# Reordering the 256-column matmuls of a split-precision decoder layer on TensorE

## The chip, the cores and the metric

The kernel runs on one core of one Trainium2 chip. The metric is the device time of one execution in microseconds (us), lower is better. Times per instruction are in nanoseconds (ns).

## The reference

One decoder layer on 256 tokens of width 2048, all in float32. Four large products carry the work, with smaller work between them:

```python
u   = x @ w_in                       # first product:  (256,2048) @ (2048,6160)
mix = concat(conv_group(u), gated_deltanet(u)) @ w_out      # second product
x   = layer_norm(alpha * x + mix)
gu  = x @ w_gate_up                  # third product:  (256,2048) @ (2048,11264)
hid = silu(gu[..., :5632]) * gu[..., 5632:]
out = layer_norm(alpha * x + hid @ w_down)                  # fourth product
```

## The kernel before

Each float32 operand of a large product is split into a rounded part `hi` and a remainder `lo`, and a product is the sum of three TensorE products: hi\*hi, hi\*lo and lo\*hi. Weights come from memory in chunks of 256 rows by 512 columns (512 KB): SyncE issues the load into `wraw` (three buffers), ScalarE copies it to `whi` (L93), VectorE subtracts to get `wlo` (L100); `whi` and `wlo` have four buffers each.

The first product is done in 12 groups of 512 output columns. A group has eight chunks, a chunk two row blocks of 128 (`k2`) and four column blocks (`ct`). The output of `ct` lies in half of a PSUM bank, 256 tokens wide, so that a group uses two banks, `g1a` and `g1b`, of a pool of four. For each row block and column block three matmuls of 256 columns follow one another into the same half bank (L206 whi with x_hi, L208 whi with x_lo, L209 wlo with x_hi): 24 matmuls a chunk. Between two chunks a planner (`tick`) places side work of the small mixers on TensorE; their times come from a table written by hand. All of it is ordered after the last matmul of the chunk (`last[0]`).

The third product is done in 22 groups (`j`) of 512 columns. The normed x is kept as `x1`, with hi and lo side by side, so that one matmul of 512 columns takes whi with both parts (L840, `g3_hi`); hi and lo land in the two halves of a whole bank, and a group has four banks, `g3a` to `g3d`. Per chunk come eight such matmuls over the four banks in turn, and then eight of 256 columns for wlo with the hi part (L849, `g3_lo`). At the end of a group ScalarE copies the lo half of each bank (L890), VectorE adds the hi half (L891), then Silu (L894), the product (L895) and the split into `hid` (L896, L897). Group 0 is a special case: its first six chunks are taken in two halves of 128 tokens, filled in around the norm and its transposes (L798), and so have 256-column matmuls at L840 too; its last two chunks are as in the other groups. The second and fourth products use matmuls of 512 columns (L715 to L717), three in a row into one bank.

Of the kernel before, what the change touches and what calls it, by code (L numbers as in the profile page):

```python
# [7 lines left out]
F32 = mybir.dt.float32  # L8
F32R = mybir.dt.float32r
AF = mybir.ActivationFunctionType  # L10
ALU = mybir.AluOpType
# [3 lines left out]
P = 128  # L15
D = 2048
S = 256
KT = D // P
# [5 lines left out]
NG3 = FF // 256  # L24
# [36 lines left out]
def hybrid_layer(ctx: ExitStack, tc, xT, xn, w1, wba, w2, w3, w4, pvec, consts, hrow, lrow, out):  # L61
    nc = tc.nc
    TT = nc.vector.tensor_tensor
    STT = nc.vector.scalar_tensor_tensor
    TS = nc.vector.tensor_scalar
    ACT = nc.scalar.activation
    MM = nc.tensor.matmul
# [9 lines left out]
    def ps(name="ps"):  # L77
        return sd.tile([P, 512], F32, tag="sd", name=name)

    def mmt(name="mmt"):  # L80
        return mm.tile([P, 512], F32, tag="mm", name=name)
# [3 lines left out]
    def wload(src, split=False, into=None):  # L85
        with tc.high_priority(offset=WPRI):
            raw = into[2] if into and len(into) > 2 else wp.tile([P, 2, 512], F32, tag="wraw", name="wraw", bufs=3)
            hi = into[0] if into else wp.tile([P, 2, 512], F32R, tag="whi", name="whi")
            lo = into[1] if into else wp.tile([P, 2, 512], F32R, tag="wlo", name="wlo")
            parts = (0, 1) if split else (slice(0, 2),)  # L90
            for k in parts:
                loads[0] = nc.sync.dma_start(raw[:, k], src[:, k])
                ACT(hi[:, k], raw[:, k], AF.Copy)  # L93
        return raw, hi, lo, parts

    def wrest(w):
        raw, hi, lo, parts = w
        with tc.high_priority(offset=WPRI):
            for k in parts:
                TT(lo[:, k], raw[:, k], hi[:, k].bitcast(F32), op=ALU.subtract)  # L100
        return hi, lo

    def wchunk(src, split=False, into=None):
        return wrest(wload(src, split, into))
# [67 lines left out]
    last = [None]  # L172
# [12 lines left out]
    def tick():  # L185
        while todo and todo[0][0] <= clock[0]:
            run_next()
        clock[0] += 1
# [7 lines left out]
    def gemm_ws(banks, chunks, r_hi, r_lo, pre=None):  # L196
        for c in range(8):
            if pre is not None:
                pre(c)
            hi, lo = wchunk(chunks[c], split=(pre is not None and c < 2))  # L200
            for k2 in range(2):
                kt = 2 * c + k2
                for ct in range(4):
                    o = banks[ct // 2][:, (ct % 2) * S:(ct % 2) * S + S]
                    wsl = slice(ct * P, ct * P + P)
                    MM(o, lhsT=hi[:, k2, wsl], rhs=r_hi[:, kt, :], start=(kt == 0 and ct % 2 == 0),  # L206
                       stop=False, skip_group_check=True)
                    MM(o, lhsT=hi[:, k2, wsl], rhs=r_lo[:, kt, :], start=False, stop=False, skip_group_check=True)  # L208
                    last[0] = MM(o, lhsT=lo[:, k2, wsl], rhs=r_hi[:, kt, :], start=False, stop=(kt == KT - 1),  # L209
                                 skip_group_check=True)  # L210
            if c < 7:
                tick()

# [207 lines left out]
    for s in (32, 64):  # L421
        for hf in range(2):
            w = pb.tile([P, 4, P], F32, name=f"wz{s}_{hf}")
# [277 lines left out]
    for gi, (kind, idx, _) in enumerate(GROUPS):  # L701
        banks = [mmt("g1a"), mmt("g1b")]
        gemm_ws(banks, w1[gi], x_hi, x_lo, pre=first_loads if gi == 0 else None)
        {"kq": do_kq, "v": do_v, "conv": do_conv, "z": do_z}[kind](banks, idx)
        if gi == 0:
            at(clock[0] + 1, gates)
        tick()
# [17 lines left out]
    def gemm2(pas, nb):  # L725
        banks = [mmt("g2a"), mmt("g2b")]
        for c in range(4):
            hi, lo = wchunk(w2[pas, nb, c])
            require(("gc"[pas], c // 2))
            for k2 in range(2):  # L730
                for tk in range(2):
                    tok_mm(banks[tk], act_c if pas else act_g, 2 * c + k2, tk, hi, lo, k2, 8)
            tick()
        return banks
# [10 lines left out]
    for nb in range(4):  # L745
        banks = gemm2(0, nb)
# [19 lines left out]
    for nb in range(2):  # L766
        banks = gemm2(1, nb)
# [3 lines left out]
    x1 = [big.tile([P, KT // 2, 2, S], F32R, tag="big", name=f"x1_{i}") for i in range(2)]  # L771
# [61 lines left out]
    def g3_banks():  # L833
        return [mmt("g3a"), mmt("g3b"), ps("g3c"), ps("g3d")]

    def g3_hi(banks, w, c, tsl):
        for k2 in range(2):
            kt = 2 * c + k2
            for ct in range(4):
                m = MM(banks[ct].rearrange("p (a b) -> p a b", a=2)[:, :, tsl], lhsT=w[:, k2, ct * P:ct * P + P],  # L840
                       rhs=x1[kt // 8][:, kt % 8, :, tsl], start=(kt == 0 and tsl.start == 0), stop=False,
                       skip_group_check=True)
        return m

    def g3_lo(banks, w, c, tsl):
        for k2 in range(2):
            kt = 2 * c + k2
            for ct in range(4):
                last[0] = MM(banks[ct][:, tsl], lhsT=w[:, k2, ct * P:ct * P + P], rhs=x1[kt // 8][:, kt % 8, 0, tsl],  # L849
                             start=False, stop=(kt == KT - 1), skip_group_check=True)  # L850

    t0, t1 = slice(0, P), slice(P, S)
    banks3 = g3_banks()
# [22 lines left out]
    p2 = ctx.enter_context(tc.tile_pool(name="p2", bufs=1))  # L876

    hid = p2.tile([P, 2, FT, S], F32R, name="hid")
    for j in range(NG3):
        banks = g3_banks() if j else banks3  # L880
        for c in range(0 if j else NF, 8):
            hi, lo = wchunk(w3[j, c])
            g3_hi(banks, hi, c, slice(0, S))
            g3_lo(banks, lo, c, slice(0, S))
        gu = []
        for i in range(2):
            g = p2.tile([P, 2, S], F32, tag="t2k2", name="g3s", bufs=5)
            for k in range(2):
                bank = banks[2 * i + k]
                ACT(g[:, k, :], bank[:, S:2 * S], AF.Copy)  # L890
                TT(g[:, k, :], g[:, k, :], bank[:, 0:S], op=ALU.add)  # L891
            gu.append(g)
        sg, hv = gu
        ACT(sg, sg, AF.Silu)  # L894
        TT(hv, sg, hv, op=ALU.mult)  # L895
        ACT(hid[:, 0, 2 * j:2 * j + 2, :], hv, AF.Copy)  # L896
        TT(hid[:, 1, 2 * j:2 * j + 2, :], hv, hid[:, 0, 2 * j:2 * j + 2, :].bitcast(F32), op=ALU.subtract)  # L897
    st2 = cp.tile([P, 2, 4, 6], F32, name="st2")
# [22 lines left out]
    for nb in range(4):  # L921
        banks = [mmt("g4a"), mmt("g4b")]
        held = 6 if nb == 3 else 0
        for c in range(NC4 - held):
            hi, lo = wchunk(w4[nb, c])
# [20 lines left out]
NF = 6  # L946
# [83 lines left out]
```

## Time and profile before

| what | value |
|---|---|
| median of 3 runs | 1180.29 us (1179.14 to 1182.05) |
| profiled execution, span from its first to its last instruction | 1178.9 us |
| TensorE matmul busy | 1161.0 us, 98% |
| TensorE weight load busy | 1033.0 us, 88% |
| VectorE busy | 763.2 us, 65% |
| ScalarE busy | 585.1 us, 50% |
| memory traffic over the span | 188 GB/s |

The profiled execution has no time of its own beside its span; the median of the runs is 1.4 us above that span. PE is TensorE's matmul row and PEld its weight load, which runs beside the matmuls. A matmul's recorded length is longer than its share of the engine, since matmuls overlap: the pace is the distance from one start to the next.

### The profile page before, as it was taken

How to read it: one execution, taken by the hardware profiler on the slowest of the kernel's cores; microseconds unless marked ns; L12 is line 12 of the kernel's file. 1: busy time of each engine (PE TensorE's matmuls, PEld its weight loads, DVE VectorE, ACT ScalarE, POOL GpSimd, SP SyncE). 2: the span in 40 equal slices, each digit the busy share in tenths (PEclk: the TensorE clock that was granted, in tenths of full speed). 3: DMA queues.
4: the chain of work that ended last, by engine and by line, in shares of the span. 5: the costliest groups of instructions: out<-in, count | busy, mean ns of one | idle time of the engine just before them, and what ended most of it. 6: DMA issues, size and time to landing. Idle time of an engine off the chain costs nothing.

```text
span 1178.9 us, 18212 instructions
## 1 busy us (share of the span) xinstructions
PE 1161.0 (98%) x7170; PEld 1033.0 (88%) x7170; DVE 763.2 (65%) x1176; ACT 585.1 (50%) x887; POOL 34.9 (3%) x44
## 2 busy tenths in 40 slices
PE   9999999999999999999999999999999999999996
PEld 8999999999988879888888888888888888888884
DVE  5998998978757687555555555555555545454546
ACT  6567555556765455454454454454444433333340
POOL 1001011000000000000000000000000000000000
PEclk9999999999999999999999999999999999999998
DMA  8667675564645746666666666666666766666662
GB/s 290 176 185 217 180 208 155 151 197 126 204 138 178 249 142 184 208 190 190 192 186 190 193 188 190 192 188 193 187 191 193 250 196 189 190 193 193 188 204 94
DMA packets 62005, 222.50 MB, mean 189 GB/s; under 512 B 7168, under 2 KB 7680, under 8 KB 61280
## 3 DMA queue, kind: packets, MB, share of 16 engines
q1 hardware_dynamic: 58464, 208.37, 58.9%
q0 software_dynamic: 2160, 10.88, 2.9%
q10 hardware_dynamic: 1296, 2.10, 0.5%
q8 instruction: 56, 0.92, 0.3%
q14 instruction: 29, 0.24, 0.1%
HBM read 216.86 MB, written 4.46 MB: 188 GB/s over the span
## 4 chain that ended last, share of the span: by engine, by line
PE 92%; DMA 4%; ACT 1%; DVE 1%; issue 1%; POOL 0%; DVEq 0%; ACTq 0%
PE g3d L840 7%; PE g3b L840 7%; PE g3c L840 7%; PE g3a L840 7%; PE g3a L849 3%; PE g1a L206 3%; PE g4b L717 3%; PE g1a L208 3%; PE g4a L717 3%; PE g1b L209 3%; PE g1a L209 3%; PE g1b L208 3%; PE g1b L206 3%; PE g4a L716 3%; PE g4b L716 3%; PE g3d L849 3%
## 5 line engine op out<-in xcount | busy, mean ns | idle before, releaser
L100 DVE TENSOR_TENSOR wlo<-wraw,whi 128x1024 fp32r<-128x1024 f32 (+1 forms) x386 | 469.8, 1218 | 367.5 <-ACT whi L93 365.7
L93 ACT ACTIVATE whi<-wraw 128x1024 fp32r<-128x1024 f32 (+1 forms) x386 | 407.0, 1055 | 490.9 <-PE g3d L840 211.5
L840 PE MATMUL g3d<-x,whi 128*128 128x512 f32 (+1 forms) x356 | 139.8, 393 | 0.0
L840 PE MATMUL g3b<-x,whi 128*128 128x512 f32 (+1 forms) x356 | 139.7, 393 | 0.0
L840 PE MATMUL g3c<-x,whi 128*128 128x512 f32 (+1 forms) x356 | 138.0, 388 | 0.0
L840 PE MATMUL g3a<-x,whi 128*128 128x512 f32 (+1 forms) x356 | 137.5, 386 | 0.0
L206 PE MATMUL g1a<-x_hi,whi 128*128 128x256 f32 x384 | 110.6, 288 | 1.1 <-ACT x_hi L143 0.6
L208 PE MATMUL g1a<-x_lo,whi 128*128 128x256 f32 x384 | 107.9, 281 | 0.1
L209 PE MATMUL g1a<-x_hi,wlo 128*128 128x256 f32 x384 | 107.5, 280 | 0.0
L206 PE MATMUL g1b<-x_hi,whi 128*128 128x256 f32 x384 | 107.5, 280 | 0.0
L209 PE MATMUL g1b<-x_hi,wlo 128*128 128x256 f32 x384 | 107.4, 280 | 0.0
L208 PE MATMUL g1b<-x_lo,whi 128*128 128x256 f32 x384 | 107.4, 280 | 0.0
L641 DVE SCALAR_TENSOR_TENSOR cacc<-hh,pv,cacc 128x255 f32<-128x255 f32 (+27 forms) x240 | 100.0, 462 | 0.7 <-ACT cacc L638 0.7
L849 PE MATMUL g3a<-x,wlo 128*128 128x256 f32 x348 | 96.9, 278 | 0.0
L849 PE MATMUL g3d<-x,wlo 128*128 128x256 f32 x348 | 96.1, 276 | 0.0
L849 PE MATMUL g3b<-x,wlo 128*128 128x256 f32 x348 | 96.0, 276 | 0.0
L849 PE MATMUL g3c<-x,wlo 128*128 128x256 f32 x348 | 96.0, 276 | 0.0
L840 PEld LDWEIGHTS g3d<-x,whi 128*128 128x128 f32 x356 | 66.9, 188 | 16.3
L840 PEld LDWEIGHTS g3c<-x,whi 128*128 128x128 f32 x356 | 66.9, 188 | 13.6
L206 PEld LDWEIGHTS g1a<-x_hi,whi 128*128 128x128 f32 x384 | 72.7, 189 | 1.8 <-ACT x_hi L143 1.0
L840 PEld LDWEIGHTS g3b<-x,whi 128*128 128x128 f32 x356 | 66.9, 188 | 8.1
L840 PEld LDWEIGHTS g3a<-x,whi 128*128 128x128 f32 x356 | 66.9, 188 | 7.5 <-DVE x L802 0.2
(307 smaller groups left out, 2129.6 us busy)
## 6 DMA issues: line engine op xcount, KB each, us to landing
wraw<-in_w SPq DMA_DIRECT2D x388, 512.0 KB, 4.2
y<-in_xn POOLq DMA_DIRECT2D x1, 2048.0 KB, 9.6
rows<-in_lrow POOLq DMA_DIRECT2D x2, 1024.0 KB, 11.6
l<-in_lrow POOLq DMA_DIRECT2D x2, 1024.0 KB, 10.3
out<-y SPq DMA_DIRECT2D x8, 256.0 KB, 2.5
xr<-in_xT ACTq DMA_DIRECT2D x7, 256.0 KB, 5.4
wraw<-in_w SPq DMA_DIRECT2D x4, 256.0 KB, 4.1
dzx<-zbg POOLq DMA_DIRECT2D x2, 512.0 KB, 5.2
```

Of the source, the lines that this page charges most:

```text
L93: ACT(hi[:, k], raw[:, k], AF.Copy)
L100: TT(lo[:, k], raw[:, k], hi[:, k].bitcast(F32), op=ALU.subtract)
L206: MM(o, lhsT=hi[:, k2, wsl], rhs=r_hi[:, kt, :], start=(kt == 0 and ct % 2 == 0), stop=False, skip_group_check=True)
L208: MM(o, lhsT=hi[:, k2, wsl], rhs=r_lo[:, kt, :], start=False, stop=False, skip_group_check=True)
L209: last[0] = MM(o, lhsT=lo[:, k2, wsl], rhs=r_hi[:, kt, :], start=False, stop=(kt == KT - 1), skip_group_check=True)
L641: STT(a[:, s:], hh[:, i, :S - s], pcol(w + TAPS - 1 - s), a[:, s:], op0=ALU.mult, op1=ALU.add)
L716: MM(bank, lhsT=a_hi[:, tsl], rhs=lo[:, k2, :], start=False, stop=False)
L717: last[0] = MM(bank, lhsT=a_lo[:, tsl], rhs=hi[:, k2, :], start=False, stop=(kt == n - 1))
L840: m = MM(banks[ct].rearrange("p (a b) -> p a b", a=2)[:, :, tsl], lhsT=w[:, k2, ct * P:ct * P + P], rhs=x1[kt // 8][:, kt % 8, :, tsl], st ...
L849: last[0] = MM(banks[ct][:, tsl], lhsT=w[:, k2, ct * P:ct * P + P], rhs=x1[kt // 8][:, kt % 8, 0, tsl], start=False, stop=(kt == KT - 1), ...
```

## The change

In the first product the 24 matmuls of a chunk are put in another order: all eight hi\*hi over the four half banks in turn, for both row blocks, then the eight hi\*lo, then the eight lo\*hi. In the third product, groups 1 to 21, the 512-column matmul is replaced by two of 256 columns in the same order, and both land in one half bank, so that a group takes two banks instead of four. With that the copies and additions at the end of a group fall away: Silu reads its bank directly, and VectorE multiplies by the other bank. Group 0 of the third product, the second and the fourth product stay as they are.

```diff
-            for k2 in range(2):
-                kt = 2 * c + k2
-                for ct in range(4):
-                    o = banks[ct // 2][:, (ct % 2) * S:(ct % 2) * S + S]
-                    wsl = slice(ct * P, ct * P + P)
-                    MM(o, lhsT=hi[:, k2, wsl], rhs=r_hi[:, kt, :], start=(kt == 0 and ct % 2 == 0),
-                       stop=False, skip_group_check=True)
-                    MM(o, lhsT=hi[:, k2, wsl], rhs=r_lo[:, kt, :], start=False, stop=False, skip_group_check=True)
-                    last[0] = MM(o, lhsT=lo[:, k2, wsl], rhs=r_hi[:, kt, :], start=False, stop=(kt == KT - 1),
-                                 skip_group_check=True)
+            for w, r, fin in ((hi, r_hi, False), (hi, r_lo, False), (lo, r_hi, True)):
+                for k2 in range(2):
+                    kt = 2 * c + k2
+                    for ct in range(4):
+                        o = banks[ct // 2][:, (ct % 2) * S:(ct % 2) * S + S]
+                        last[0] = MM(o, lhsT=w[:, k2, ct * P:ct * P + P], rhs=r[:, kt, :],
+                                     start=(kt == 0 and ct % 2 == 0 and r is r_hi and not fin),
+                                     stop=(fin and kt == KT - 1), skip_group_check=True)
...
+    def g3_evac(banks):
+        sg = p2.tile([P, 2, S], F32, tag="t2k2", name="g3s", bufs=5)
+        ACT(sg.rearrange("p a b -> p (a b)"), banks[0], AF.Silu)
+        hv = p2.tile([P, 2, S], F32, tag="t2k2", name="g3h", bufs=5)
+        return sg, banks[1].rearrange("p (a b) -> p a b", a=2), hv
+
+    def g3_chunk(banks, hi, lo, c):
+        for w, part, fin in ((hi, 0, False), (hi, 1, False), (lo, 0, True)):
+            for k2 in range(2):
+                kt = 2 * c + k2
+                for ct in range(4):
+                    last[0] = MM(banks[ct // 2][:, (ct % 2) * S:(ct % 2) * S + S], lhsT=w[:, k2, ct * P:ct * P + P],
+                                 rhs=x1[kt // 8][:, kt % 8, part, :],
+                                 start=(kt == 0 and ct % 2 == 0 and part == 0 and not fin),
+                                 stop=(fin and kt == KT - 1), skip_group_check=True)
+
+    for j in range(NG3):
+        banks = [mmt("g3a"), mmt("g3b")] if j else banks3
+        for c in range(0 if j else NF, 8):
+            hi, lo = wchunk(w3[j, c])
+            if j:
+                g3_chunk(banks, hi, lo, c)
+            else:
+                g3_hi(banks, hi, c, slice(0, S))
+                g3_lo(banks, lo, c, slice(0, S))
+        sg, up, hv = g3_evac(banks) if j else g3_evac0(banks)
+        TT(hv, sg, up, op=ALU.mult)
```

`g3_evac0` is the old end of a group, kept for group 0.

## Rows read from the trace of the kernel before

**Rows 1.** The page: span, busy time of each engine, granted TensorE clock in 40 slices.

```profile
span 1178.9 us, 18212 instructions
PE 1161.0 (98%) x7170; PEld 1033.0 (88%) x7170; DVE 763.2 (65%) x1176; ACT 585.1 (50%) x887; POOL 34.9 (3%) x44
PEclk9999999999999999999999999999999999999998
```

**Rows 2.** Window of groups 1 to 21 of the third product: length, PE busy, clock, DMA.

```profile
459.80:925.72 465.92, 465.92 (x2690) 1.00 0.67 195
```

**Rows 3.** Timeline of PE, one chunk of the third product: start us, recorded length us.

```profile
601.24 0.39 PE L840 MATMUL g3a<-x,whi 128*128 128x512 f32 x1
601.47 0.40 PE L840 MATMUL g3b<-x,whi 128*128 128x512 f32 x1
601.71 0.39 PE L840 MATMUL g3c<-x,whi 128*128 128x512 f32 x1
...
603.11 0.28 PE L849 MATMUL g3a<-x,wlo 128*128 128x256 f32 x1
603.22 0.28 PE L849 MATMUL g3b<-x,wlo 128*128 128x256 f32 x1
...
604.02 0.39 PE L840 MATMUL g3a<-x,whi 128*128 128x512 f32 x1
```

**Rows 4.** Timeline of PE, first product: first matmuls of two chunks, seven chunks apart.

```profile
40.05 0.28 PE L206 MATMUL g1a<-x_hi,whi 128*128 128x256 f32 x1
...
59.09 0.28 PE L206 MATMUL g1a<-x_hi,whi 128*128 128x256 f32 x1
```

**Rows 5.** The same, another stretch: first matmuls of two chunks, twelve chunks apart.

```profile
117.10 0.28 PE L206 MATMUL g1a<-x_hi,whi 128*128 128x256 f32 x1
...
151.02 0.28 PE L206 MATMUL g1a<-x_hi,whi 128*128 128x256 f32 x1
```

**Rows 6.** Groups of PE in 37.5 to 64.6 us: busy us, mean ns | idle.

```profile
L209 PE MATMUL g1a<-x_hi,wlo 128*128 128x256 f32 x40 | 11.0, 276 | 0.0
```

**Rows 7.** Groups of PE in 114.5 to 156.8 us.

```profile
L209 PE MATMUL g1a<-x_hi,wlo 128*128 128x256 f32 x60 | 16.9, 281 | 0.0
```

**Rows 8.** Groups over the whole span, shapes apart: busy us, mean ns | idle.

```profile
L208 PE MATMUL g1b<-x_lo,whi 128*128 128x256 f32 x384 | 107.4, 280 | 0.0
L849 PE MATMUL g3b<-x,wlo 128*128 128x256 f32 x348 | 96.0, 276 | 0.0
```

**Rows 9.** Timeline of PE, group 0 of the third product, 256-column matmuls over four banks.

```profile
444.09 0.28 PE L840 MATMUL g3b<-x,fxhi 128*128 128x256 f32 x1
...
445.73 0.28 PE L849 MATMUL g3d<-x,fxlo 128*128 128x256 f32 x1
```

**Rows 10.** The same, later in group 0; 32 matmuls from first to last.

```profile
450.63 0.28 PE L840 MATMUL g3a<-x,whi 128*128 128x256 f32 x1
...
454.26 0.39 PE L840 MATMUL g3a<-x,whi 128*128 128x512 f32 x1
```

**Rows 11.** Timeline of PE, first product, chunks that follow side work, two cases.

```profile
103.50 0.28 PE L209 MATMUL g1a<-x_hi,wlo 128*128 128x256 f32 x1
...
103.97 0.28 PE L206 MATMUL g1b<-x_hi,whi 128*128 128x256 f32 x1
...
110.47 0.28 PE L209 MATMUL g1a<-x_hi,wlo 128*128 128x256 f32 x1
...
110.92 0.28 PE L206 MATMUL g1b<-x_hi,whi 128*128 128x256 f32 x1
```

**Rows 12.** Chain that ended last, in order of time, in 160 to 170 us.

```profile
163.37 1.78 PE pw L434 x16
```

**Rows 13.** Waits in 455 to 926 us: us in total, times, longest.

```profile
ACT whi L93 <- PE g3d L840: 211.5, 144, 2.0
DVE wlo L100 <- ACT whi L93: 204.5, 168, 1.8
```

**Rows 14.** Groups in 460 to 925 us, end of a group of the third product.

```profile
L891 DVE TENSOR_TENSOR g3s<-g3s,g3d 128x256 f32<-128x256 f32 x21 | 8.7, 416 | 0.0
L890 ACT ACTIVATE g3s<-g3d 128x256 f32<-128x256 f32 x21 | 8.3, 395 | 0.0
```

**Rows 15.** Timeline of all engines, start of the first product.

```profile
12.45 0.38 PE L206 MATMUL g1a<-x_hi,whi 128*128 128x256 f32 x1 [0.23 <-ACT x_hi L143]
12.90 0.38 PE L208 MATMUL g1a<-x_lo,whi 128*128 128x256 f32 x1
```

More of the change, by code (lines that the diff above doesn't have):

```diff
@@ L878, in hybrid_layer, with g3_evac0 @@
     hid = p2.tile([P, 2, FT, S], F32R, name="hid")
[L879 to L884, printed above, removed]
+    def g3_evac0(banks):
         gu = []
@@ L894, in hybrid_layer @@
         ACT(sg, sg, AF.Silu)
-        TT(hv, sg, hv, op=ALU.mult)
+        return sg, hv, hv
+    def g3_evac(banks):
[23 more added lines that the diff above has]
+        TT(hv, sg, up, op=ALU.mult)
         ACT(hid[:, 0, 2 * j:2 * j + 2, :], hv, AF.Copy)
```

## The prediction

> **What bounds the kernel now.** I read the page first: TensorE's matmul row is busy for 98% of the span and its clock is granted in full in every slice but the last [rows 1], the upper of its two levels (2.4 GHz). So the time is a sum of matmul paces, and a change counts by what it does to the distance from one matmul start to the next. The waits of the third product have no TensorE in them: ScalarE waits until TensorE has released a weight buffer, VectorE waits for ScalarE [rows 13]. The weights are ahead of TensorE, and neither transfers nor splits bound that stage.
>
> Then the timeline of one chunk of the third product. Its eight 512-column matmuls take from 601.24 to 603.11 us, 234 ns each; its eight 256-column ones from 603.11 to 604.02, 114 ns each [rows 3]. The wide matmul is dearer per column: 234 against 2 x 114 = 228. The whole stage gives the exact figure: 465.92 us [rows 2] over 21 groups of eight chunks, 168 chunks, is 2.773 us a chunk.
>
> Then two stretches of the first product, where 256-column matmuls run alone, 24 a chunk, all loading a weight tile each. From 40.05 to 59.09 us seven chunks pass, 2.720 us each, 113.3 ns a matmul [rows 4]. From 117.10 to 151.02 twelve chunks pass, 2.827 us each, 117.8 ns a matmul [rows 5]. The same code has **two paces**, 4.5 ns apart. The recorded length tells them apart: 276 ns in the quick stretch [rows 6], 281 in the slow one [rows 7]. Inside each stretch the pace does not change for 168 and 288 matmuls. It changes where side work or a stall comes in between: two chunks that both follow side work settle differently, one with four steps in 0.47 us, 118 ns each (103.50 to 103.97), the other with four in 0.45, 113 ns (110.47 to 110.92) [rows 11].
>
> So I don't read the slow pace as the price of adding three times into one region. In the quick stretch three matmuls in a row also add into one region; and in group 0 of the third product, where the output goes over four banks in turn, both paces occur: 444.09 to 445.73 us holds 14 steps of 117 ns [rows 9], 450.63 to 454.26 holds 32 of 113.4 [rows 10]. Order does not fix the pace; how the stream of matmuls starts does.
>
> **The change, part by part.**
>
> *Third product, matmuls.* 1344 matmuls of 512 columns (8 x 168) go, 2688 of 256 come; a chunk has 24 matmuls of 256 columns. No row shows this stage so, so I bound it: at the quick pace 2.720 us a chunk, at the slow one 2.827, against 2.773. That is 168 x (2.720 - 2.773) = -9.0 us, or 168 x (2.827 - 2.773) = +9.0 us. I take the quick pace. After each burst of 512-column matmuls the 256-column ones fall into it at once (their mean length over the run is 276 ns at the second bank [rows 8]); group 0 ends with such a burst, so group 1 starts quick; nothing is placed on TensorE between groups 1 and 21; and TensorE waits for nothing there.
>
> *Weight loads.* 24 a chunk instead of 16. Side work of 128-column matmuls, each with its own load, passes in 1.78 us for 16, 111 ns each [rows 12], so a load needs no more than 111 ns and lies beside a 113.3 ns matmul. It costs nothing, which is what rows 4 show with the same 24 loads. The cover is thin, 2 ns: if a load took 114 it would cost 0.7 x 24 x 168 = 2.8 us.
>
> *Third product, end of a group.* Four copies of 395 ns on ScalarE and four additions of 416 ns on VectorE [rows 14] go, 21 times: about 33 and 35 us of work off engines at 50% and 65% [rows 1]. Silu and the product now read PSUM. I cost this at nothing: the next group's two banks are another pair of the pool of four, and a group lasts 22 us. Without that cover the end of a group would cost Silu and product, about 1 us each time by the rows for half that width (395 and 416 ns). SyncE's loads, ScalarE's copies and VectorE's subtractions for weights keep their number; in each chunk whi is released after 16 of 24 matmuls, 1.81 us, before it was 1.87 [rows 3].
>
> *First product, steady part.* Same 2304 matmuls, same shapes. The share at the slow pace comes from the mean length: 107.4 us over 384 is 279.7 ns, between 276 and 281 [rows 6 to 8], so 0.74. All quick would save 0.74 x 2304 x 4.5 ns = 7.7 us, all slow would cost 0.26 x 2304 x 4.5 = 2.7 us. Side work still comes between chunks and still resets the pace, so I keep the share: 0, with -7.7 and +2.7 as bounds.
>
> *First product, start.* x arrives piece by piece. x_lo is now wanted eight matmuls (0.9 us) after x_hi, instead of one. The third chunk lost 0.45 - 0.11 = 0.34 us there [rows 15]. Against that, the first chunk wants its second half of x and weights after four matmuls rather than twelve, 0.9 us sooner; the next piece of x holds TensorE up afterwards anyway, so I count that as covered. I take -0.4 us, between -1 and +0.9. The evacuation of a group's first bank starts four matmuls (0.5 us) later; the next group uses two other banks, so TensorE does not wait.
>
> *Sum.* 1178.9 - 9.0 - 0.4 = 1169.5 us of span. The median of the runs is 1.4 us above the span, so 1170.9 us.
>
> **The rivals.**
>
> *The rotation makes the first product quick too.* It would be so if the new order helped the stream to settle after side work. For: among the few starts over four banks in group 0 quick ones occur [rows 10]. Against: a slow stretch in the same rotation [rows 9], and quick ones in the old order [rows 4]. Time: 1170.9 - 7.7 = 1163.2 us.
>
> *The third product locks into the slow pace.* The 512-column matmuls that reset the pace are gone, so a single late weight or a hiccup could throw the stream into the slow pace, and with no side work to throw it out again it would stay for the rest of 457 us. For: the slow stretch of the first product lasted all of rows 5. Against: TensorE shows no wait in that stage. Fully locked: 1180.3 + 9.0 - 0.4 = 1188.9 us. It decides from half of the stage on: half at 2.827 and half at 2.720 is 2.773, no gain.
>
> *The excess is per stream, and each matmul has a price of its own.* If the 234 ns came from this stage's operands rather than from the width, pairs would pay it too. Then nothing is gained, and at the slow pace's excess a pair costs 235.6 - 233.8 = 1.8 ns more than now, 1344 x 1.8 = 2.4 us: 1180 to 1182.7. Rows 3 and 4 speak against it: two quick 256-column matmuls take 7 ns less than one of 512. The Trainium skill, TensorE: Matmul & The Clock Gate, section Back-to-back issue gap, has a rule on this side: a warm matmul is spaced by its columns over 2.4 GHz plus about 2.5 ns, so narrower matmuls pay that more often. By that rule, 1344 more matmuls would cost 3.4 us and the time would be about 1183; the trace disagrees, with 113.3 and 234 ns where the rule gives 109.2 and 215.8.
>
> **How the numbers follow.** Forecast (third quick, first as mixed as now) 0.52; its own range, with the slow share of the first moved by 0.3 (3.1 us), is 1167.5 to 1174.5. First quick as well: 0.19. Third at the slow pace wholly or in part: 0.17, spread over 1172 to 1189. Excess stays: 0.07. Something else between 1172 and 1182 (a stall at a group's end, a dearer start): 0.05. The range 1162 to 1184 leaves out the fully locked case and the edges, some 0.15. A measurement of this kernel tells about 0.3%, 3.5 us, from no change. Faster takes the first two cases and a little of the others: 0.76. Same: most of the excess case, a half-locked third and the rest: 0.10. Slower: the locked case from well over half on: 0.14.
>
> **What would show it.** In the new profile the third product's groups 1 to 21 should last 457 us, with lengths of 276 ns on all three kinds of matmul; 281 would mean the locked case. TensorE should show no wait there, and the lines L890 and L891 should have one group's entries left. The first product should still mix 276 and 281, with changes of pace only at side work; a mean near 276 would be the rotation rival. The second and fourth products should last as before. The prediction is wrong if the pace slips without anything on TensorE in between, since all of it rests on the pace holding.

## The result, and the profile after

The changed kernel takes 1171.74 us (median of 4 runs, 1170.69 to 1173.28) against 1180.93 us before (4 runs, 1179.14 to 1182.05): ratio 0.9929, 95% interval 0.9917 to 0.994. 1170.9 was predicted. The profiled span fell by 7.4 us, from 1178.9 to 1171.5, and the median by 9.2 us: the profiled execution of the changed kernel is the slowest of its four, whose spans go from 1168.9 to 1171.5 us.

The page of the changed kernel, its span, busy times and granted clock, answers to [rows 1].

```profile
span 1171.5 us, 20710 instructions
PE 1153.6 (98%) x8514; PEld 1087.4 (93%) x8514; DVE 735.6 (63%) x1092; ACT 561.3 (48%) x803; POOL 34.9 (3%) x44
PEclk9999999999999999999999999999999999999998
```

1344 more matmuls and as many more loads, and yet 7.4 us less matmul time: the bound is still TensorE's pace, and the clock is the same. Where the time went shows in two windows of the changed kernel (length, PE busy, clock, DMA share, GB/s): groups 1 to 21 of the third product, and the last group of the first product with the side work behind it.

```profile
461.29:918.25 456.96, 456.96 (x4035) 1.00 0.59 200
302.36:334.22 31.86, 31.07 (x269) 1.00 0.61 215
```

The first answers to [rows 2]: 456.96 us in place of 465.92, 9.0 less, 2.720 us a chunk. The second lasted 30.40 us before, with TensorE busy all through:

```profile
302.70:333.10 30.40, 30.40 (x269) 1.00 0.65 217
```

So -8.96 and +1.46 make -7.5. All the other stretches together come to +0.1 us; they differ by up to 0.4 us each, and cancel.

The groups of PE over the whole span in the changed kernel (busy us, mean ns of one | idle) show the paces.

```profile
L901 PE MATMUL g3b<-x,whi 128*128 128x256 f32 x1344 | 261.7, 276 | 0.0
L901 PE MATMUL g3b<-x,wlo 128*128 128x256 f32 x672 | 130.8, 276 | 0.0
L206 PE MATMUL g1b<-x_lo,whi 128*128 128x256 f32 x384 | 76.5, 281 | 0.0
```

Groups 1 to 21 of the third product have the 276 ns of the quick pace [rows 6]. The first product, in its new order, still has the mixed mean of the old one [rows 8].

At the end of a group of the third product Silu and product now read PSUM, and TensorE does not wait for them.

```profile
L916 DVE TENSOR_TENSOR g3h<-g3s,g3b 128x512 f32<-128x512 f32 x21 | 14.3, 680 | 0.0
L892 ACT ACTIVATE g3s<-g3a 128x512 f32<-128x512 f32 x21 | 12.2, 579 | 0.0
```

The copies and additions of [rows 14] are gone from groups 1 to 21; the waits of PE between 461 and 918 us are an empty list.

The 1.5 us that were lost lie in the last group of the first product. The timeline there starts ten microseconds earlier, with `f`, a scale factor of the mixers: VectorE begins it, GpSimd (POOL) finishes it, and ScalarE multiplies by it (L586; L588 in the kernel before). Rows of VectorE, ScalarE and PE, changed kernel:

```profile
292.60 1.22 DVE L100 TENSOR_TENSOR wlo<-wraw,whi 128x1024 fp32r<-128x1024 f32 x1
293.73 0.17 DVE L581 SCALAR_TENSOR_TENSOR f<-sso,fe 128x8 f32<-128x8 f32 x1
295.83 0.40 ACT L586 ACTIVATE vs<-vs,f 128x128 f32<-128x128 f32 x1 [2.86 <-POOL f L583]
...
302.25 1.28 ACT L599 ACT_TABLE_LOAD   x1
303.54 0.60 ACT L599 ACTIVATE sz<-g1a 128x512 f32<-128x512 f32 x1
304.04 0.59 ACT L599 ACTIVATE sz<-g1b 128x512 f32<-128x512 f32 x1
304.64 1.08 ACT L481 COPY early<-pz 32x128 f32<-32x128 f32 x4
305.22 0.38 PE L432 MATMUL pw<-early 128*128 128x128 f32 x1 [0.79 <-ACT early L481]
```

The same in the kernel before:

```profile
292.64 0.17 DVE L583 SCALAR_TENSOR_TENSOR f<-sso,fe 128x8 f32<-128x8 f32 x1
293.86 1.23 DVE L100 TENSOR_TENSOR wlo<-wraw,whi 128x1024 fp32r<-128x1024 f32 x1
294.75 2.16 ACT L588 ACTIVATE vs<-vs,f 128x128 f32<-128x128 f32 x7 [1.21 <-POOL f L585]
...
300.36 1.28 ACT L601 ACT_TABLE_LOAD   x1
301.65 0.60 ACT L601 ACTIVATE sz<-g1a 128x512 f32<-128x512 f32 x1
303.10 0.59 ACT L601 ACTIVATE sz<-g1b 128x512 f32<-128x512 f32 x1
303.70 1.08 ACT L483 COPY early<-pz 32x128 f32<-32x128 f32 x4
304.85 1.95 PE L434 MATMUL pw<-early 128*128 128x128 f32 x16
```

In the changed kernel VectorE splits a chunk of weights ahead of `f` and not behind it, so that `f` comes 1.1 us later: 0.7 behind that split, 0.4 because the sums that it needs end later on ScalarE. ScalarE waits for it, and all that stands behind it there is late: its first multiplication by 1.08 us, the four copies that the side work needs (`early`) by 0.94. TensorE reaches the side work, in the middle of a chunk, and waits 0.79 us at L432.

By these rows the lateness does not come from Silu's banks; ScalarE is late before it reaches Silu. The last matmul into the group's first bank ends at 301.50 us, before it was 301.40, and in both kernels Silu starts only when ScalarE's table load is over. Silu of the first bank is 1.9 us late because a weight copy now goes ahead of it that before stood behind it; Silu of the second bank and the copies `early` are as late as ScalarE already was. This is read from the two traces (and from those of `first_only` and `third_only` below, which agree); no run moves the split alone. What put the weight work further ahead in these queues is not shown; `whi` is released earlier in the new order, and that may be the reason.

The wait is 0.79 of the 1.46 us. The 32 side-work matmuls right behind it, whose first half reads those copies, take 3.83 us (305.22 to 309.05) in place of 3.49 (304.85 to 308.34), 0.34 more; the remaining 0.3 us are spread over the rest of the window.

### The profile page after: what moved, and what is told of

Its sections match the earlier page's. It is cut to its first block, busy times and chain, and to the rows that moved or that the text cites. A ratio compares the mean times of both kernels' runs of the same rounds, so it can differ in the third digit from the quotient of the medians.

```text
span 1171.5 us, 20710 instructions
## 1 busy us (share of the span) xinstructions
PE 1153.6 (98%) x8514; PEld 1087.4 (93%) x8514; DVE 735.6 (63%) x1092; ACT 561.3 (48%) x803; POOL 34.9 (3%) x44
## 3 DMA queue, kind: packets, MB, share of 16 engines
q8 instruction: 66, 1.08, 0.4%
## 4 chain that ended last, share of the span: by engine, by line
PE 71%; ACT 1%; DVE 1%; issue 1%; DMA 1%; POOL 0%; DVEq 0%; ACTq 0%
PE g3b L901 20%; PE g3a L901 20%; PE g4b L715 3%; PE g4a L715 3%; PE g4a L714 3%; PE g4b L714 3%; PE g4b L713 3%; PE g4a L713 3%; PE g1a L206 1%; PE g1b L206 1%; PE g2a L715 1%; PE g2a L713 1%; PE g2b L713 1%; PE g2a L714 1%; PE g2b L715 1%; PE g2b L714 1%
## 5 line engine op out<-in xcount | busy, mean ns | idle before, releaser
L901 PE MATMUL g3b<-x,whi 128*128 128x256 f32 x1344 | 261.7, 276 | 0.0
L901 PE MATMUL g3a<-x,whi 128*128 128x256 f32 x1344 | 261.6, 276 | 0.0
L901 PEld LDWEIGHTS g3a<-x,whi 128*128 128x128 f32 x1344 | 202.3, 188 | 0.0
L901 PEld LDWEIGHTS g3b<-x,whi 128*128 128x128 f32 x1344 | 202.3, 188 | 0.0
L901 PEld LDWEIGHTS g3a<-x,wlo 128*128 128x128 f32 x672 | 101.2, 188 | 0.0
L901 PEld LDWEIGHTS g3b<-x,wlo 128*128 128x128 f32 x672 | 101.1, 188 | 0.0
L715 PE MATMUL g4b<-whi,hid 128*128 128x512 f32 x172 | 67.8, 394 | 0.0
L715 PE MATMUL g4a<-whi,hid 128*128 128x512 f32 x172 | 67.8, 394 | 0.0
L714 PE MATMUL g4a<-wlo,hid 128*128 128x512 f32 x172 | 67.4, 392 | 0.0
L714 PE MATMUL g4b<-wlo,hid 128*128 128x512 f32 x172 | 67.4, 392 | 0.0
L713 PE MATMUL g4a<-whi,hid 128*128 128x512 f32 x172 | 66.8, 388 | 0.0
```

The source lines that it names most:

```text
L713: MM(bank, lhsT=a_hi[:, tsl], rhs=hi[:, k2, :], start=(kt == 0), stop=False)
L714: MM(bank, lhsT=a_hi[:, tsl], rhs=lo[:, k2, :], start=False, stop=False)
L715: last[0] = MM(bank, lhsT=a_lo[:, tsl], rhs=hi[:, k2, :], start=False, stop=(kt == n - 1))
L901: last[0] = MM(banks[ct // 2][:, (ct % 2) * S:(ct % 2) * S + S], lhsT=w[:, k2, ct * P:ct * P + P], rhs=x1[kt // 8][:, kt % 8, part, :], st ...
```

## The experiments

**The change in halves.** `third_only` has the third product changed and the first in its old order; `first_only` the reverse. Each diff is one half of the change's own.

> The third product as in the changed kernel, the first product in its old order. Theory (the wide matmuls of the third product were the whole gain, the order in the first product is worth nothing): groups 1 to 21 last 457.0 us, the first product mixes both paces as before, its last group is 1.2 us shorter than in the changed kernel, and the time is 9 us below before, 1171 to 1172 us, so level with or 1 us below the changed kernel. Rival (the rotation helps the first product, and its gain was eaten elsewhere): 2 us or more above the changed kernel.

> The first product in the new order, the third as before. Theory: no gain; the same chunks run at 113 and 118 ns a matmul as before, the start gains 0.1 to 0.4 us, the last group loses 1.2 us to a later Silu, so 0 to 1.5 us above before. Rival (rotation over regions quickens 256-column matmuls): 5 to 8 us below before.

`third_only`: 1170.19 us, ratio 0.9916 (0.9902 to 0.993). `first_only`: 1180.71 us, ratio 1.0005 (0.9996 to 1.0015). The windows of the last group of the first product are, for `first_only` and then for `third_only`:

```profile
302.84:334.76 31.92, 31.14 (x269) 1.00 0.64 215
```

```profile
303.16:333.56 30.40, 30.40 (x269) 1.00 0.63 220
```

and the wait of PE in 300 to 335 us of `first_only` is

```profile
PE pw L432 <- ACT early L481: 0.8, 1, 0.8
```

The gain is the third product's alone. The new order of the first product has no measurable worth: it does not move its mean pace, and it is what brings the wait at L432. The loss there is 1.5 us, where 1.2 was expected; that a later Silu causes it, as both expectations say, is not borne out: in `first_only` too ScalarE waits 2.85 us for `f`, until 296.30 us. `first_only` comes out 0.4 us above before and not 1.5: a stretch at the start of the first product was quicker in its profiled execution, and the interval holds both.

**Order inside the third product.** `third_in_row` is `third_only` with the three products of a column block in a row:

```diff
-        for w, part, fin in ((hi, 0, False), (hi, 1, False), (lo, 0, True)):
-            for k2 in range(2):
-                kt = 2 * c + k2
-                for ct in range(4):
+        for k2 in range(2):
+            kt = 2 * c + k2
+            for ct in range(4):
+                for w, part, fin in ((hi, 0, False), (hi, 1, False), (lo, 0, True)):
```

> As third_only, but the 24 matmuls of a chunk of the third product in the old order of the first: hi*hi, hi*lo and lo*hi in a row into one region. Theory (width counts, order does not): groups 1 to 21 last 457.0 us at 113.3 ns a matmul, same time as third_only. Rival (adding three times in a row into one region is what costs 118 ns): 168 chunks at 2.827 us, 475 us, 18 us above third_only.

1169.99 us, ratio 0.9913 (0.99 to 0.9927), the time of `third_only`. Groups 1 to 21 in its window:

```profile
457.86:914.82 456.96, 456.96 (x4034) 1.00 0.61 199
```

That is the same 456.96 us to a hundredth. Adding three times in a row into one region costs nothing here, and the rotation is not what made the third product quick.

What no run separates is width from place. The fourth product has 512-column matmuls too, three in a row into one bank, and there they pass more quickly than 234 ns. Timeline of PE in the kernel before:

```profile
999.88 0.39 PE L715 MATMUL g4a<-whi,hid 128*128 128x512 f32 x1
...
1001.26 0.39 PE L715 MATMUL g4a<-whi,hid 128*128 128x512 f32 x1
```

These are six steps in 1.38 us, 230 ns each. By the starts over the whole product, the step is 226 ns behind L715, 229 behind L716 and 232 behind L717, 229 in the mean. In the third product it is 228 behind `g3a`, 231 behind `g3c` and 236 behind `g3b` and `g3d`, 233 in the mean (the one chunk of [rows 3] gives 234). So a wide matmul can pass in 226 ns, the time of a quick pair. Had the 1344 of the third product passed in 229, about 5 of the 9 us would have been gained without splitting them. Whether another order of the wide matmuls over their banks would do that was not tried.

**Does the pace hold, and can it slip?** `third_disturbed` puts other work on TensorE in the third product.

```diff
+            if j in (4, 14) and c == 0:
+                with tc.issue_after(last[0].ins):
+                    for scr in (ps("scr"), ps("scr")):
+                        for i in range(4):
+                            last[0] = TR(scr[:, i * P:i * P + P], ones, ident)
+            if j == 9 and c == 0:
+                with tc.issue_after(last[0].ins):
+                    scr = ps("scr")
+                    last[0] = MM(scr, lhsT=x1[0][:, 0, 0, 0:P], rhs=x1[0][:, 0, :, :].rearrange("p a b -> p (a b)"),
+                                 start=True, stop=True)
```

> As third_only, with eight transposes of 128 columns into a scratch bank ahead of groups 4 and 14 of the third product, and one 512-column matmul into a scratch bank ahead of group 9; the output stays the reference's. Theory (the pace is kept until something else comes on TensorE, transposes put it to slow, a wide matmul puts it back): groups 4 to 8 and 14 to 21 at 2.827 us a chunk, the others at 2.720; 13 x 8 x 0.107 = 11 us above third_only. Rival (the order of the third product holds the quick pace by itself): only the transposes' own 2 us above third_only.

1177.94 us, one run, 7.8 above `third_only`. Groups of PE in 523 to 632 us (groups 4 to 8) and in 742 to 922 us (groups 14 to 21):

```profile
L903 PE MATMUL g3b<-x,whi 128*128 128x256 f32 x320 | 62.3, 276 | 0.0
...
L903 PE MATMUL g3b<-x,whi 128*128 128x256 f32 x512 | 102.2, 281 | 0.0
```

The first transposes left the stream quick, the second ones threw it into the slow pace, and there it stayed to the end of the product: 64 chunks at +0.107 us are 6.8 us, the 16 transposes at 0.11 us 1.8 and the wide matmul 0.2, together 8.8. The 21 groups lasted 465.8 us (457.11 to 922.94) in place of 457.0. So the locked case of the rivals is a real danger and was only not met. That transposes always bring the slow pace, as I had expected, is refuted.

`third_disturbed_64` adds a matmul of 64 columns behind each set of transposes:

```diff
+                    MM(banks[0][:, 0:64], lhsT=x1[0][:, 0, 0, 0:P], rhs=x1[0][:, 0, 0, 0:64], start=True, stop=True)
```

> third_disturbed with a 64-column matmul between the eight transposes and the first matmul of groups 4 and 14. Theory (how the stream starts sets the pace, and a narrow matmul in between makes it quick): groups 4 to 8 and 14 to 21 all at 2.720 us a chunk, 7 us below third_disturbed, about 1171 us. Rival (transposes in the third product make it slow whatever follows): groups 14 to 21 stay at 2.827, 1178 us.

1177.90 us, one run, but with the paces changed over. The groups of PE in 526 to 639, 639 to 748 and 749 to 922 us:

```profile
L903 PE MATMUL g3b<-x,whi 128*128 128x256 f32 x320 | 63.8, 281 | 0.0
```

```profile
L903 PE MATMUL g3b<-x,whi 128*128 128x256 f32 x320 | 62.3, 276 | 0.0
...
L903 PE MATMUL g3b<-x,whi 128*128 128x256 f32 x512 | 99.6, 276 | 0.0
```

Now groups 4 to 8 are slow and 14 to 21 quick, and the slow stretch ends at the 512-column matmul ahead of group 9. The narrow matmul does not choose the quick pace here; with it, each of the two places came out the other way. The time is the rival's 1178, but not by its paces: groups 14 to 21 are quick.

**The first product's pace.** Three kernels add a matmul with a zero weight tile, which adds zero, after side work in the first product. `first_reset_512` and `first_reset_64` put it ahead of the chunk, 512 or 64 columns wide, and `first_mid_512` in the middle of the chunk.

```diff
+            if ran[0] and last[0] is not None:
+                ran[0] = False
+                MM(banks[0][:, 0:64], lhsT=zt, rhs=r_hi[:, 0, 0:64], start=(c == 0), stop=False, skip_group_check=True)
```

> As third_only, with one 512-column matmul of a zero weight tile, adding zero to the group's first bank, after each piece of side work in the first product. Theory (a wide matmul puts the stream into the quick pace, whatever came before): the slow share of the first product falls from 0.74 to below 0.1, 7 us gained, about 35 wide matmuls at 0.23 us lost, so within 2 us of third_only, and the lengths on the three lines of the first product go to 276 ns. Rival (something else in the first product, its operands or the traffic beside it, makes it slow): the lengths stay at 280 and the time is 8 us above third_only.

> The same with the zero matmul 64 columns wide. Theory (any change in how the stream starts draws the pace anew): other chunks than before are quick and slow, the share is open; the matmuls themselves cost at most 35 x 0.11 = 4 us. Rival (the pace of a chunk depends on the chunk): the same chunks as in third_only are slow.

> As first_reset_512, but the 512-column zero matmul stands in the middle of the chunk that follows side work, after 12 of its 24 matmuls, so inside a running stream of loads and matmuls. Theory (a wide matmul inside the stream always brings the quick pace, as at group 9 of third_disturbed_64, while the start after side work draws either pace): the slow share of the first product falls to about 0.2, the half chunks ahead of the wide ones; about 34 x 0.23 = 8 us lost, 5 to 6 us gained, 2 to 3 us above third_only. Rival (a wide matmul only draws anew): as in first_reset_512, a share near 0.3 with stretches of both paces behind the wide ones.

`first_reset_512` took 1173.79, `first_reset_64` 1170.33 and `first_mid_512` 1178.99 us, one run each, against 1170.19 of `third_only`. The groups of PE in 34 to 332 us (to 335 for the last) of `third_only`, `first_reset_64`, `first_reset_512` and `first_mid_512`, in this order:

```profile
L208 PE MATMUL g1b<-x_lo,whi 128*128 128x256 f32 x352 | 98.5, 280 | 0.0
```

```profile
L215 PE MATMUL g1b<-x_lo,whi 128*128 128x256 f32 x352 | 97.3, 276 | 0.0
```

```profile
L215 PE MATMUL g1b<-x_lo,whi 128*128 128x256 f32 x348 | 96.7, 278 | 0.0
```

```profile
L216 PE MATMUL g1b<-x_lo,whi 128*128 128x256 f32 x346 | 96.7, 279 | 0.0
```

With 64 columns ahead of the chunk nearly the whole first product ran quick; that it is not bound to the slow pace is shown. No time was gained by it: 35 added matmuls at 0.11 us and a wait of 1.1 us at L385 stood against the pace, the first product ended 1.2 us sooner, and what follows up to the third product lasted 1.4 us longer. With 512 ahead, stretches of both paces changed places. By the recorded lengths 0.31 of the matmuls were slow, where the theory had less than 0.1 and its rival the old 0.7; both are refuted. In the middle of the chunk 0.69 were slow, where about 0.2 was expected: the wide matmul also turned quick streams slow, against my theory. The timeline of PE in `first_mid_512` shows one:

```profile
117.18 0.28 PE L214 MATMUL g1b<-x_hi,whi 128*128 128x256 f32 x1
...
117.52 0.39 PE L208 MATMUL g1a<-x_hi,zt 128*128 128x512 f32 x1
117.75 0.28 PE L214 MATMUL g1a<-x_hi,whi 128*128 128x256 f32 x1
...
118.45 0.28 PE L214 MATMUL g1b<-x_hi,whi 128*128 128x256 f32 x1
```

Three steps of 113 ns lead up to it; after it six steps take 0.70 us, 117 ns each.

Without added matmuls the pace of most stretches of the first product is not a matter of chance. From 95 us to the last group 27 stretches lie between two pieces of side work, and within none of them does the pace change. Each has the same pace in all eight kernels that add nothing to the first product, the changed kernel and `first_only` with the new order among them. Two neighbours, in 201.2 to 206.4 and in 208.6 to 213.6 us, in the kernel before and then in the changed one:

```profile
L208 PE MATMUL g1b<-x_lo,whi 128*128 128x256 f32 x8 | 2.2, 276 | 0.0
L208 PE MATMUL g1b<-x_lo,whi 128*128 128x256 f32 x8 | 2.2, 281 | 0.0
```

```profile
L206 PE MATMUL g1b<-x_lo,whi 128*128 128x256 f32 x8 | 1.6, 276 | 0.0
L206 PE MATMUL g1b<-x_lo,whi 128*128 128x256 f32 x8 | 1.6, 281 | 0.0
```

Only ahead of 95 us do some stretches differ from kernel to kernel.

**Versions that beat both.** `third_fourth` also splits the fourth product's matmuls over the two halves of their bank:

```diff
+        for a_, w, fin in ((a_hi, hi, False), (a_hi, lo, False), (a_lo, hi, True)):
+            for h in range(2):
+                hs = slice(h * S, h * S + S)
+                last[0] = MM(bank[:, hs], lhsT=a_[:, tsl], rhs=w[:, k2, hs],
+                             start=(kt == 0 and h == 0 and a_ is a_hi and w is hi),
+                             stop=(fin and kt == n - 1), skip_group_check=True)
```

> As third_only, and each 512-column matmul of the fourth product as two of 256 columns over the two halves of its bank. Theory (a wide matmul costs 229 ns here, two quick narrow ones 226.7, and the quick pace comes in from the third product and stays): 1056 pairs, 2.5 us below third_only. Rival (the fourth product's wide matmuls carry little excess and the pairs lose the quick pace at a group's end or pay for double loads): level or up to 9 us above third_only.

1169.04 us, ratio 0.9904 (0.9889 to 0.9919). The windows of the fourth product to the end, `third_only` and then `third_fourth`:

```profile
915.11:1168.38 253.27, 241.93 (x1058) 0.98 0.55 182
```

```profile
916.27:1167.60 251.33, 240.27 (x2114) 0.98 0.56 184
```

1.9 us shorter, where 2.5 were expected; the medians differ by 1.2 us, and their intervals overlap.

`third_fourth_reset` adds the 64-column matmul to that, only where no side work follows the chunk (20 places).

> third_fourth with the 64-column zero matmul in the first product, only after side work that is followed by two or more chunks without any: 20 of them. Theory (the narrow matmul makes the stream start quick): most of the first product's slow stretches go, 4 to 5 us gained, 20 x 0.11 = 2.2 us lost, so 2 to 3 us below third_fourth, about 1166.5 us. Rival (the quick chunks of the run before were luck of one execution): the slow share stays near 0.7 and the time is 2 us above third_fourth.

1165.96 us, ratio 0.9883 (0.9867 to 0.99): the best time of the study, 14 us below before. The groups of PE in 34 to 329 us:

```profile
L215 PE MATMUL g1b<-x_lo,whi 128*128 128x256 f32 x352 | 97.6, 277 | 0.0
```

Most of the first product ran quick again, in another execution and with fewer narrow matmuls, so this was not the luck of one run; but one of the 20 places (37.8 to 65.8 us) came out slow. Past the start of the first product, 52 of the 54 stretches behind a 64-column matmul ran quick in the two kernels.

## Why the prediction was right, point by point

*Third product, matmuls.* The forecast of the quick pace and of -9.0 us held: 456.96 us against 457. The wide matmuls of this product took 233 ns in the mean, a quick pair takes 226.7, and neither the order nor the regions of the pairs count (`third_in_row`). That width alone makes 233 is not shown: the same width passes in 226 to 232 ns in the fourth product. The pace held for 4032 matmuls, with nothing else on TensorE; `third_disturbed` shows what the rival would have cost. That the pace would be the quick one was rightly forecast, but a given start can bring either, as `third_disturbed_64` shows.

*Weight loads.* Costed at nothing, and the stage shows nothing of them.

*End of a group of the third product.* Costed at nothing; no wait of TensorE.

*First product, steady part.* The share of the slow pace was kept at 0.74, and the means stayed at 280 to 281 ns. The longest slow stretch, 114 to 157 us, was slow again; but the stretch of [rows 4] turned slow and the one after it quick. That the rotation would make the first product quick, the first rival, is refuted by `first_only`.

*First product, start.* -0.4 us was taken; the eleventh group starts 0.35 us earlier than before (at 271.02 against 271.37 us), but the second only 0.14 us (33.59 against 33.73), and the rest is stretches that changed their pace. From execution to execution the start of the first product differs by more: its second group begins between 33.6 and 35.0 us in the profiles of this study. So the term is neither confirmed nor refuted.

*The sum.* It adds 1.4 us from the span to the time; in every execution that has both, the time is 1.7 to 1.9 us above the span, so this term was 0.4 us short. That the median came within 0.8 us of the forecast is in part luck: the lost 1.5 us were not in the sum, and by the profiled executions, whose span is 2.0 us above the forecast one, the miss is larger.

*The step that failed* is that the first product was costed by its matmuls alone: 0 for its steady part, and "TensorE does not wait" for the bank that is evacuated half a microsecond later. The banks were free, and that half microsecond did no harm. But the new order also moved the weight work in the queues of VectorE and ScalarE. `f` came 1.1 us later, the side work's copies 0.94, and the last group lost 1.5 us, which `third_only` does not lose (its window has the 30.40 us of before). The medians, 1170.19 against 1171.74 us, come from separate comparisons with overlapping intervals and do not settle it by themselves.

*The rival with a price of each matmul* has no support: groups 1 to 21 have twice as many matmuls for the wide part, and the time fell by just what the pace says. Its first half is in part true, since about 4 of the 233 ns belong to this product's place (229 in the fourth), but the pairs did not pay them. The Trainium skill, TensorE: Matmul & The Clock Gate, section Back-to-back issue gap, gives the rule of columns over 2.4 GHz plus 2.5 ns for an isolated matmul and says that it is off in a stream of loads and matmuls. So the prediction should not have held it against this stream, and its failure here (113.3 and 234 ns against 109.2 and 215.8) does not contradict the page.

*Open.* What sets the pace. Shown are two steady paces for the same instructions, that a stream keeps its pace, over 4032 matmuls the quick one and over 1536 the slow one, until something else comes in between, that a matmul of another width or a few transposes can turn it either way, and that from 95 us on the same stretch of the first product takes the same pace from kernel to kernel where nothing is added. Neither width, order, regions nor the kind of side work decides by itself: behind the same two kinds (`pkk`, `pgb`) one stretch is quick (110 us) and the next slow (114 us) in all eight kernels. That the exact time at which loads and matmuls meet decides is the theory that is left; it was not shown. Open too is why wide matmuls take 226 to 236 ns by their place.

## What to carry to other kernels

Measure the distance from start to start of a matmul by width, in the place where it will stand, before choosing the width: in the third product two of 256 columns were cheaper than one of 512 by 6 ns, in the fourth by 2, though they load their weights twice. Where streams of equal matmuls show two paces, don't put the slower one down to their order before the same order has been seen at both. When the order of the matmuls changes, follow the queues of the other engines too, and who stands behind the work that moves there, not only the buffers.

## What was not expected of the hardware

The same stream of loads and matmuls of 256 columns runs at 113.3 or at 117.8 ns a matmul, for 4032 and for 1536 matmuls on end, at the full granted clock, and one 512-column matmul in between took it from quick to slow in the first product and from slow to quick in the third. Which pace a stretch of the first product takes repeats in eight kernels for all 27 stretches from 95 us on. A matmul of 64 columns with a load of its own cost 0.11 us and, put after side work in the first product, left nearly all of it at the quick pace.
